# Six modulation vectors of a two-block network made in earlier stages

## The chip, the cores and the metric

The kernel runs on one core of a Trainium2 chip. The metric is the device time of one execution in microseconds (us); lower is better. TensorE is called PE in the views, VectorE DVE, ScalarE ACT, GpSimd POOL and SyncE SP.

## What is computed

512 tokens of 1024 channels, batch 1, go through two blocks of two layers each. Every layer is modulated by vectors that come from one conditioning row: `cond @ w` with a 1024 x 1024 piece of a weight matrix for each vector. They don't depend on the tokens, so each can be made at any time before its use.

```python
def first_block(...):                    # layer 0: even_mixer (MLA and window), layer 1: odd_mixer (diff and forgetting)
    cond = jax.nn.silu(c)
    for layer in range(DEPTH):           # DEPTH = 2
        mod = cond @ w_ada[layer] + b_ada[layer]
        shift, scale, gate = jnp.split(mod, 3, axis=-1)
        h = rmsnorm(x, g_pre[layer]) * (1.0 + scale[:, None, :]) + shift[:, None, :]
        y = even_mixer(h, ...) if layer % 2 == 0 else odd_mixer(h, ...)
        x = x + gate[:, None, :] * rmsnorm(y, g_post[layer])
    return x

def second_block(...):                   # layer 0: conformer_conv, layer 1: hgrn2_mixer
    cond = jax.nn.silu(c)
    for i in range(DEPTH):
        mod = (cond @ ada_w[i] + ada_b[i]).astype(x.dtype)
        sh1, sc1, g1, sh2, sc2, g2 = jnp.split(mod, 6, axis=-1)
        h = modulate(rms_norm(x, norm1_g[i]), sh1, sc1)
        y = conformer_conv(h, ...) if i % 2 == 0 else hgrn2_mixer(h, ...)
        x = x + g1[:, None, :] * y
        h = modulate(rms_norm(x, norm2_g[i]), sh2, sc2)
        a = jax.nn.relu(h @ mlp_w1[i])   # 1024 x 4096
        x = x + g2[:, None, :] * ((a * a) @ mlp_w2[i])
    return rms_norm(x, final_g)
```

## The kernel before

The stages follow one another: even attention, odd attention, convolution, first MLP, recurrent mixer ("hgrn"), second MLP. All activations stay in SBUF, transposed, as a pair of high and low parts (`hTh`, `hTl`); a product in float32 is the sum of three products of such parts (`mm3`, lines 206 to 208). Weights are loaded by SyncE in granules of 512 KB (`wgran`, lines 210 to 226, the load at line 214). They go into one of four `raw` buffers and are split into one of five `hl` buffers: the high part on ScalarE (line 222), the low part on VectorE or GpSimd (line 225). The MLP goes through four quarters of 1024 hidden units. A quarter is w1 and then w2. w1 is done by `gemm_q`, which multiplies in seven block products instead of eight: it sums weight blocks (line 1211), splits them (lines 200 and 201), multiplies (line 1231), and VectorE adds the products (line 1224). w2 is done by plain products, and VectorE multiplies their sums by the gate (line 1145). The first half of quarter 0's w1 is done by plain products, too.

A modulation vector is made by `ada` (line 485) in eight steps, four for each half of its 1024 columns. A step loads 512 KB of the weight matrix (line 495, on SyncE's queue) into one of two buffers `araw`, or in the recurrent stage into one of the four `raw`. One step later VectorE multiplies and adds them into `acc` in two operations of 128 x 512 (line 546, the first of a half line 544). After four steps TensorE sums `acc` over the partitions in a block of eight small products (line 552). VectorE adds the bias (line 554) and, for a scale or a gate with a norm weight, one more operation (line 507), and SyncE writes the half to DRAM in four rows (line 510). In the convolution TensorE does the products itself. Where a vector is used, `spread` (line 588) loads it for all partitions.

`ada` only puts the eight steps on the list `pend`. `group` (line 571) is called for every finished group of outputs, and at every `tick_every`-th call it takes one step from the list; `flush` (line 581) takes all that are left. A scheduler then sets the order of each engine's instructions. It may place a step's instructions earlier than where they were issued, as far as buffers and a marked gate allow. Each engine and each queue does its list in order.

The lines that the change touches are in `first` (the odd attention), `second` (convolution and recurrent stage), `mlp` and the part of `build` ahead of the first MLP. Other names: in the attentions line 637 reads scores into the softmax, line 640 is its reciprocal, line 644 GpSimd's scaling, lines 623 and 625 are rope, line 709 adds a part of the output `o`, line 204 splits a transposed part `b`, and line 654 transposes. In the recurrent stage `X` (lines 1593 and 1596) is a step of the scan.

## Time and profile before

| | |
|---|---|
| runs, median of 3 | 2077.5 us (2074.36 to 2078.72) |
| the profiled execution, its own time | 2076.88 us |
| its span in the profile | 2075.1 us |
| mean granted clock of TensorE | 0.969 of full speed |
| TensorE busy | 1950.8 us, 94% of the span |
| VectorE busy | 1322.0 us, 64% |
| ScalarE, GpSimd busy | 881.2 us (42%), 741.7 us (36%) |
| bytes moved by DMA | 272.13 MB |

The span is the time from the first to the last instruction in the trace; it is 1.8 us shorter than the execution's own time. Stages, from the lines of their instructions: odd attention to about 700 us, with its mixer from 407 to 690; convolution to about 985; first MLP from there to 1336; recurrent stage to about 1700; second MLP from about 1711 to the end. Of a window the columns are its length, then the busy time (and number of instructions) of PE, PEld (weight loads of TensorE), DVE, ACT and POOL, the granted clock of TensorE as a share of its upper level, the busy share of DMA, and GB/s.

### The profile page before, as it was taken

How to read it: one execution, taken by the hardware profiler on the slowest of the kernel's cores; microseconds unless marked ns; L12 is line 12 of the kernel's file. 1: busy time of each engine (PE TensorE's matmuls, PEld its weight loads, DVE VectorE, ACT ScalarE, POOL GpSimd, SP SyncE). 2: the span in 40 equal slices, each digit the busy share in tenths (PEclk: the TensorE clock that was granted, in tenths of full speed). 3: DMA queues.
4: the chain of work that ended last, by engine and by line, in shares of the span. 5: the costliest groups of instructions: out<-in, count | busy, mean ns of one | idle time of the engine just before them, and what ended most of it. 6: DMA issues, size and time to landing. Idle time of an engine off the chain costs nothing.

```text
span 2075.1 us, 33235 instructions
## 1 busy us (share of the span) xinstructions
PE 1950.8 (94%) x13047; PEld 1591.7 (77%) x13047; DVE 1322.0 (64%) x1976; ACT 881.2 (42%) x1497; POOL 741.7 (36%) x671
## 2 busy tenths in 40 slices
PE   7799999699999999879899999999999998999998
PEld 5687767677766787448788989877787678898896
DVE  4356674467553369646988658557677858475673
ACT  3345543135543441142525436244566534353452
POOL 1233344233233233005232422446586543323222
PEclk9899979899999999999999999999999999999999
DMA  8484456377761335832554234452423422242331
GB/s 309 135 211 154 134 163 167 80 176 165 117 148 51 134 116 184 225 88 92 175 169 146 80 113 153 141 158 88 117 75 114 133 82 82 82 133 72 122 103 60
DMA packets 229972, 272.13 MB, mean 131 GB/s; under 512 B 26810, under 2 KB 154009, under 8 KB 229816
## 3 DMA queue, kind: packets, MB, share of 16 engines
q1 hardware_dynamic: 192054, 232.83, 38.9%
q10 hardware_dynamic: 37762, 37.18, 6.1%
q8 instruction: 103, 1.69, 0.3%
q14 instruction: 53, 0.43, 0.1%
HBM read 253.57 MB, written 16.40 MB: 130 GB/s over the span
## 4 chain that ended last, share of the span: by engine, by line
PE 46%; DVE 8%; issue 4%; DMA 3%; ACT 1%; POOL 1%; ACTq 0%; POOLq 0%; SPq 0%; DVEq 0%
PE mm L208 26%; PE mm L1231 5%; PE sc L208 4%; PE sc L1231 4%; PE tp L1231 3%; DVE ol L1351 2%; DMA ud<-u 1%; DVE hl L201 1%; DVE acc L546 1%; PE pv L208 1%; DVE hl L225 1%; DMA u<-ud 1%; PE tp L609 0%; POOL xr L1756 0%; PE sc L1370 0%
## 5 line engine op out<-in xcount | busy, mean ns | idle before, releaser
L208 PE MATMUL mm<-hTh,hl 128*128 128x512 f32 (+2 forms) x1200 | 371.7, 384 | 0.1
L222 ACT CAST hl<-raw 128x1024 fp32r<-128x1024 f32 (+3 forms) x219 | 224.2, 1034 | 238.5 <-PE mm L208 117.8
L208 PE MATMUL mm<-hl,hid 128*128 128x512 f32 x1344 | 317.2, 395 | 3.6 <-DVE hid L201 2.0
L208 PEld LDWEIGHTS mm<-hl,hid 128*128 128x128 f32 x1344 | 251.8, 188 | 63.5 <-DVE hid L201 3.0
L225 DVE TENSOR_TENSOR hl<-raw,hl 128x1024 fp32r<-128x1024 f32 (+2 forms) x187 | 243.1, 1309 | 55.6 <-ACT hl L222 47.7
L208 PEld LDWEIGHTS mm<-hTh,hl 128*128 128x128 f32 (+1 forms) x1200 | 218.0, 188 | 48.7 <-issue 6.5
L208 PE MATMUL mm<-hl,hTh 128*128 128x256 f32 (+3 forms) x848 | 218.5, 339 | 29.2 <-DVE t L625 21.2
L208 PE MATMUL mm<-hTl,hl 128*128 128x512 f32 (+2 forms) x600 | 229.4, 383 | 0.1
L1148 POOL TENSOR_TENSOR xr<-xr,t 128x512 f32<-128x512 f32 x56 | 80.7, 1441 | 306.3 <-DVE t L1145 304.5
L208 PEld LDWEIGHTS mm<-hl,hTh 128*128 128x128 f32 x848 | 152.0, 200 | 46.6 <-issue 15.8
L644 POOL TENSOR_TENSOR s<-s,sm 128x256 f32<-128x256 f32 (+3 forms) x112 | 81.2, 726 | 200.3 <-DVE sm L640 193.0
L546 DVE SCALAR_TENSOR_TENSOR acc<-araw,ccol,acc 128x512 f32<-128x512 f32 x154 | 134.5, 873 | 26.7 <-DMA araw<-in_ada_w_dram 20.7
L200 ACT CAST hl<-raw 128x1024 fp32r<-128x1024 f32 x84 | 86.9, 1048 | 138.3 <-PE mm L208 111.9
L208 PE MATMUL mm<-hl,hTl 128*128 128x256 f32 (+3 forms) x424 | 142.4, 336 | 0.6 <-DVE hTl L458 0.6
L201 DVE TENSOR_TENSOR hl<-raw,hl 128x1024 fp32r<-128x1024 f32 x84 | 131.4, 1579 | 13.7 <-ACT hl L200 13.1
L208 PEld LDWEIGHTS mm<-hTl,hl 128*128 128x128 f32 (+1 forms) x600 | 113.1, 189 | 21.8 <-issue 1.4
L1211 POOL TENSOR_TENSOR raw<-raw,raw 128x1024 f32<-128x1024 f32 x28 | 77.0, 2749 | 142.9 <-DVE rows L1211 89.0
L225 POOL TENSOR_TENSOR hl<-raw,hl 128x1024 fp32r<-128x1024 f32 x32 | 79.4, 2483 | 100.8 <-ACT hl L222 100.8
L639 ACT ACTIVATE s<-s,sm 128x256 f32<-128x256 f32 (+5 forms) x128 | 69.6, 543 | 90.6 <-DVE sm L637 83.5
L1145 DVE TENSOR_TENSOR t<-mm,rows 128x512 f32<-128x512 f32 x56 | 38.5, 688 | 107.4 <-PE mm L208 107.1
L208 PE MATMUL sc<-b,b 64*128 64x256 f32 (+7 forms) x384 | 92.0, 356 | 1.7 <-DVE sm L637 1.2
L1596 POOL TENSOR_TENSOR X<-X,T 128x512 f32<-128x512 f32 x56 | 75.8, 1358 | 44.6 <-ACT op L1556 32.1
(366 smaller groups left out, 4036.0 us busy)
## 6 DMA issues: line engine op xcount, KB each, us to landing
raw<-in_mlp_w_dram SPq DMA_DIRECT2D x128, 512.0 KB
araw<-in_ada_w_dram SPq DMA_DIRECT2D x72, 512.0 KB
raw<-in_hgrn_w_in_dram SPq DMA_DIRECT2D x40, 512.0 KB
araw<-in_w_ada_dram SPq DMA_DIRECT2D x32, 512.0 KB
raw<-in_od_w_in_dram SPq DMA_DIRECT2D x32, 512.0 KB
raw<-in_ada_w_dram SPq DMA_DIRECT2D x24, 512.0 KB
rows<-row SPq DMA_DIRECT2D x16, 512.0 KB
raw<-in_conv_w_in_dram SPq DMA_DIRECT2D x16, 512.0 KB
```

The source lines that it names most:

```text
L200: nc.scalar.copy(out=hi, in_=src)
L201: nc.vector.tensor_tensor(out=lo, in0=src, in1=hi.bitcast(F32), op=ALU.subtract)
L208: self.nc.tensor.matmul(out, lhsT=lt[a], rhs=rt[b], start=start and n == 0, stop=stop and n == 2)
L222: self.nc.scalar.copy(out=hi, in_=raw[:, :n])
L225: eng.tensor_tensor(out=lo, in0=raw[:, :n], in1=hi.bitcast(F32), op=ALU.subtract)
L546: eng.scalar_tensor_tensor(out=acc, in0=raw[:, k], scalar=c, in1=acc, op0=ALU.mult, op1=ALU.add)
L639: nc.scalar.activation(out=s[:, :m], in_=s[:, :m], func=AF.Exp, scale=-1.0, bias=mn, accum_out=sm)
L644: nc.gpsimd.tensor_tensor(out=p, in0=p, in1=r.to_broadcast([P, n]), op=ALU.mult)
L1148: eng.tensor_tensor(out=xs, in0=xs, in1=t, op=ALU.add)
L1211: eng.tensor_tensor(out=out, in0=x, in1=y, op=f)
L1231: nc.tensor.matmul(ps[:, m * 256:m * 256 + 256], lhsT=ws[n][:, a, k, m * P:m * P + P], rhs=parts[n][b][:, k], start=m + k + t == 0, stop=m ...
L1596: nc.gpsimd.tensor_tensor(out=xk, in0=xk, in1=cap(Tt, 1, [(row - 1, 2), (2, nb), (0, hh)]), op=ALU.mult)
```

## The change

The three vectors of the recurrent mixer (scale, shift and gate of `wa2[1]`, 24 steps) were on the list of the first MLP. They are put on that of the odd attention, which then has seven vectors instead of four. There a step is now taken at every finished group instead of every second (`TO`). The three vectors of the second MLP (scale, shift and gate, 24 steps) were on the list of the recurrent stage; they are put on that of the first MLP. There no step is taken during quarter 0, and one at every second group from quarter 1 on. The list isn't flushed at the MLP's end: four steps are left to the recurrent stage.

```diff
@@ -55,7 +55,7 @@
 TE = 2
 NP = 24
 G2 = 2
-TO = 2
+TO = 1
 SQ = 3
 TV = 0
 TVE = 3
@@ -1254,6 +1254,7 @@
         nc = self.nc
         for q in range(4):
             hid = {}
+            self.tick_every = 2 if q else 1000
 
             def pair(n):
                 if n not in hid:
@@ -1679,6 +1680,9 @@
                         rows += [k.ada(cc2, wa2[0], ba2[0], 1024, "scale", h["norm1_g_2"][0]),
                                  k.ada(cc2, wa2[0], ba2[0], 0, "shift")]
                         mods[0] = [k.ada(cc2, wa2[0], ba2[0], 2048, "gate")]
+                        mods["n1"] = [k.ada(cc2, wa2[1], ba2[1], 1024, "scale", h["norm1_g_2"][1]),
+                                      k.ada(cc2, wa2[1], ba2[1], 0, "shift")]
+                        mods[1] = [k.ada(cc2, wa2[1], ba2[1], 2048, "gate")]
                     if G2 == 2 + i:
                         mods["g2"] = k.ada(cc2, wa2[0], ba2[0], 5120, "gate")
                     o = mixer(act)
@@ -1710,12 +1714,10 @@
                 k.ada_tag = "tq"
                 k.ada_raw = ("raw", 4) if i else ("araw", 2)
                 k.tick_every = 1
-                if i == 0 or AH:
+                if i == 0:
                     rest(i)
                 if i == 0 and G2 == 4:
                     mods["g2"] = k.ada(cc2, wa2[0], ba2[0], 5120, "gate")
-                if i and AH > 1:
-                    mods[1] += [k.ada(cc2, wa2[1], ba2[1], 5120, "gate")]
                 k.tick_every = TE if i else 1
                 k.ada_pe, k.ada_ps = i == 0, "tp"
                 o = mixer(act)
@@ -1771,23 +1773,17 @@
                 if MK & 2:
                     k.mark()
                 g2 = mods["g2"] if G2 else k.ada(cc2, wa2[0], ba2[0], 5120, "gate")
-                rows = [k.ada(cc2, wa2[1], ba2[1], 1024, "scale", h["norm1_g_2"][1]),
-                        k.ada(cc2, wa2[1], ba2[1], 0, "shift")]
-                mods[1] = [k.ada(cc2, wa2[1], ba2[1], 2048, "gate")]
-                if AH < 1:
-                    rest(1)
-                if AH < 2:
-                    mods[1] += [k.ada(cc2, wa2[1], ba2[1], 5120, "gate")]
+                rest(1)
+                mods[1] += [k.ada(cc2, wa2[1], ba2[1], 5120, "gate")]
                 st = {}
 
                 def last(tb):
                     if tb == 0:
-                        k.flush()
-                        st["S"], st["B"] = [k.spread(r) for r in rows]
+                        st["S"], st["B"] = [k.spread(r) for r in mods["n1"]]
                     nc.scalar.dma_start(out=(out if upto == 4 else x4)[tb * P:(tb + 1) * P, :], in_=xr[tb])
                     k.prenorm(k.act, tb, xr[tb], st["S"], st["B"])
 
-                k.mlp(act, h["mlp_w1_2"][0], h["mlp_w2_2"][0], xr, lambda: k.tick(len(k.pend) - NP) or k.spread(g2), last)
+                k.mlp(act, h["mlp_w1_2"][0], h["mlp_w2_2"][0], xr, lambda: k.spread(g2), last)
             if upto == 4:
                 return
         with tc.tile_pool(name="xp", bufs=1, reuse_waits="tile") as k.xp:
```

How the order moves, at three places, all on VectorE.

At the start of the odd attention, ahead of its first output part `o` (line 709) and the first split of a transposed part `b` (line 204), before the change:

```order
L554 TENSOR_TENSOR arow_4109<-mm_4111,arow_4109 128x128
L544 TENSOR_SCALAR acc_4104<-araw_4105,ccol_93 128x512
...
L546 SCALAR_TENSOR_TENSOR acc_4104<-araw_4105,ccol_93,acc_4104 128x512
L546 SCALAR_TENSOR_TENSOR acc_4104<-araw_4176,ccol_93,acc_4104 128x512 x2
L546 SCALAR_TENSOR_TENSOR acc_4104<-araw_4321,ccol_93,acc_4104 128x512
...
L546 SCALAR_TENSOR_TENSOR acc_4104<-araw_4321,ccol_93,acc_4104 128x512
L546 SCALAR_TENSOR_TENSOR acc_4104<-araw_4449,ccol_93,acc_4104 128x512 x2
...
L709 SCALAR_TENSOR_TENSOR o_4180<-o_4180,mm_4294 128x512
...
L204 SCALAR_TENSOR_TENSOR b_972_4246<-tq_4241,b_972_4246 128x512
```

And after it, at the same place:

```order
L544 TENSOR_SCALAR acc_4113<-araw_4114,ccol_93 128x512
...
L546 SCALAR_TENSOR_TENSOR acc_4113<-araw_4114,ccol_93,acc_4113 128x512
L546 SCALAR_TENSOR_TENSOR acc_4113<-araw_4159,ccol_93,acc_4113 128x512 x2
...
L546 SCALAR_TENSOR_TENSOR acc_4113<-araw_4189,ccol_93,acc_4113 128x512 x2
L546 SCALAR_TENSOR_TENSOR acc_4113<-araw_4219,ccol_93,acc_4113 128x512 x2
...
L544 TENSOR_SCALAR acc_4281<-araw_4282,ccol_93 128x512
...
L546 SCALAR_TENSOR_TENSOR acc_4281<-araw_4282,ccol_93,acc_4281 128x512
L546 SCALAR_TENSOR_TENSOR acc_4281<-araw_4384,ccol_93,acc_4281 128x512
...
L546 SCALAR_TENSOR_TENSOR acc_4281<-araw_4384,ccol_93,acc_4281 128x512
L709 SCALAR_TENSOR_TENSOR o_4223<-o_4223,mm_4357 128x512
...
L546 SCALAR_TENSOR_TENSOR acc_4281<-araw_4481,ccol_93,acc_4281 128x512
...
L204 SCALAR_TENSOR_TENSOR b_990_4309<-tq_4304,b_990_4309 128x512
```

Four loads (`araw`) are summed ahead of line 709 before, and ten after; the first four of the ten make up a half that stands ahead of the rows shown. Ahead of line 204 it is four before and twelve after, the twelfth with one of its two operations.

In w1 of the first MLP's quarter 1, before, where `hl` are split weights, `hid` split hidden units, `t` the sums of products:

```order
L1224 TENSOR_TENSOR t_2047_9958<-t_2047_9958,tp_10012 128x512
L554 TENSOR_TENSOR arow_10048<-tq_10050,arow_10048 128x128
L544 TENSOR_SCALAR acc_10043<-araw_10044,ccol_93 128x512
L201 TENSOR_TENSOR hl_10200<-raw_10190,hl_10200 128x1024
L546 SCALAR_TENSOR_TENSOR acc_10043<-araw_10044,ccol_93,acc_10043 128x512
L1211 TENSOR_TENSOR rows_10198<-raw_10194,raw_10196 128x1024
L1224 TENSOR_TENSOR t_2048_9959<-t_2048_9959,mm_10060 128x512
L201 TENSOR_TENSOR hid_10040<-t_2047_9958,hid_10040 128x2x256
L546 SCALAR_TENSOR_TENSOR acc_10043<-araw_10117,ccol_93,acc_10043 128x512
L1224 TENSOR_TENSOR t_2047_9958<-t_2048_9959,sc_10086 128x512
L546 SCALAR_TENSOR_TENSOR acc_10043<-araw_10117,ccol_93,acc_10043 128x512
L546 SCALAR_TENSOR_TENSOR acc_10043<-araw_10152,ccol_93,acc_10043 128x512
```

And after:

```order
L201 TENSOR_TENSOR hl_10253<-raw_10243,hl_10253 128x1024
L1211 TENSOR_TENSOR rows_10251<-raw_10247,raw_10249 128x1024
L1224 TENSOR_TENSOR t_2067_10034<-t_2067_10034,mm_10121 128x512
L201 TENSOR_TENSOR hid_10115<-t_2066_10033,hid_10115 128x2x256
L1224 TENSOR_TENSOR t_2066_10033<-t_2067_10034,sc_10147 128x512
L1224 TENSOR_TENSOR t_2067_10034<-t_2067_10034,tp_10178 128x512 x2
L201 TENSOR_TENSOR hid_10175<-t_2066_10033,hid_10175 128x2x256
L201 TENSOR_TENSOR hl_10258<-raw_10243,hl_10258 128x1024
```

The operations of lines 544, 546 and 554 that stood among the splits and sums are gone from this place.

In w1 of quarter 3, after; before, no modulation operation stands there:

```order
L1224 TENSOR_TENSOR t_2250_11617<-t_2250_11617,tp_11671 128x512
L554 TENSOR_TENSOR arow_11707<-tq_11709,arow_11707 128x128
L544 TENSOR_SCALAR acc_11702<-araw_11703,ccol_93 128x512
L201 TENSOR_TENSOR hl_11851<-raw_11841,hl_11851 128x1024
L546 SCALAR_TENSOR_TENSOR acc_11702<-araw_11703,ccol_93,acc_11702 128x512
L1211 TENSOR_TENSOR rows_11849<-raw_11845,raw_11847 128x1024
L1224 TENSOR_TENSOR t_2251_11618<-t_2251_11618,mm_11719 128x512
L201 TENSOR_TENSOR hid_11699<-t_2250_11617,hid_11699 128x2x256
L546 SCALAR_TENSOR_TENSOR acc_11702<-araw_11807,ccol_93,acc_11702 128x512
L1224 TENSOR_TENSOR t_2250_11617<-t_2251_11618,sc_11745 128x512
L546 SCALAR_TENSOR_TENSOR acc_11702<-araw_11807,ccol_93,acc_11702 128x512
L546 SCALAR_TENSOR_TENSOR acc_11702<-araw_11960,ccol_93,acc_11702 128x512
```

A half's sums now stand among the splits and sums of quarter 3: these, and three more of line 546 behind them.

## Rows read from the trace of the kernel before

**Rows 1.** The page, part 1: busy time, share of the span and count of each engine.

```profile
PE 1950.8 (94%) x13047; PEld 1591.7 (77%) x13047; DVE 1322.0 (64%) x1976; ACT 881.2 (42%) x1497; POOL 741.7 (36%) x671
```

**Rows 2.** Windows of both MLPs: busy (count) by engine, then clock, DMA share, GB/s.

```profile
992.20:1021.90 29.70, 24.17 (x178) 22.86 (x176) 29.70 (x31) 16.49 (x20) 5.99 (x3) 0.89 0.51 162
1021.90:1070.50 48.60, 46.54 (x208) 36.27 (x209) 38.53 (x47) 14.29 (x19) 16.11 (x9) 1.00 0.57 184
1070.50:1118.80 48.30, 44.19 (x353) 42.71 (x352) 46.26 (x52) 25.37 (x34) 14.49 (x4) 0.93 0.58 180
1118.80:1164.00 45.20, 45.20 (x201) 36.28 (x200) 22.10 (x26) 12.29 (x15) 15.25 (x10) 1.00 0.26 85
1249.10:1289.50 40.40, 40.40 (x338) 40.36 (x337) 36.39 (x36) 24.18 (x33) 10.72 (x4) 1.00 0.48 158
1740.90:1768.40 27.50, 22.53 (x171) 22.12 (x170) 26.18 (x25) 18.49 (x25) 7.24 (x3) 0.88 0.37 115
1768.40:1813.00 44.60, 44.60 (x195) 36.16 (x193) 17.67 (x21) 12.17 (x15) 15.14 (x10) 1.00 0.23 71
1813.00:1852.90 39.90, 39.90 (x338) 39.90 (x337) 36.12 (x36) 24.73 (x34) 10.63 (x4) 1.00 0.44 133
```

**Rows 3.** Windows of the first MLP, line 546 alone: VectorE busy (count).

```profile
992.20:1021.90 29.70, 6.56 (x6) 0.89 0.51 162
1021.90:1070.50 48.60, 18.62 (x20) 1.00 0.57 184
1070.50:1118.80 48.30, 9.85 (x11) 0.93 0.58 180
```

**Rows 4.** Windows of the odd, the even and the recurrent stage, columns as in 2.

```profile
407.00:690.00 283.00, 273.87 (x1540) 205.91 (x1540) 157.15 (x369) 127.29 (x263) 94.48 (x83) 0.99 0.58 126
150.00:330.00 180.00, 174.62 (x1042) 129.06 (x1039) 125.60 (x328) 90.47 (x245) 58.59 (x104) 0.91 0.55 154
1336.00:1690.00 354.00, 347.61 (x3265) 272.76 (x3264) 245.49 (x317) 183.69 (x275) 199.06 (x158) 1.00 0.39 119
```

**Rows 5.** Waits of PE, recurrent stage: us in total, times, longest.

```profile
PE tp L1577 <- POOL X L1596: 1.5, 2, 0.9
PE tp L1586 <- DVE X L1593: 1.3, 2, 0.8
```

**Rows 6.** PE by line, line 552, recurrent stage and odd attention.

```profile
L552 PE MATMUL tq<-acc,ones 128*32 128x128 f32 x48 | 3.8, 285 | 0.0
...
L552 PE MATMUL mm<-acc,ones 128*32 128x128 f32 x64 | 3.8, 285 | 0.0
```

**Rows 7.** DVE by line, recurrent stage: busy, mean ns, idle before.

```profile
L546 DVE SCALAR_TENSOR_TENSOR acc<-raw,ccol,acc 128x512 f32<-128x512 f32 x42 | 41.8, 996 | 16.1 <-DMA raw<-in_ada_w_dram 15.5
```

**Rows 8.** DVE by line, odd attention, columns as in 7.

```profile
L546 DVE SCALAR_TENSOR_TENSOR acc<-araw,ccol,acc 128x512 f32<-128x512 f32 x49 | 41.4, 844 | 19.3 <-DMA araw<-in_ada_w_dram 15.0 <-DMA araw<-in_w_ada_dram 4.0
...
L544 DVE TENSOR_SCALAR acc<-araw,ccol 128x512 f32<-128x512 f32 x7 | 6.9, 990 | 0.0
```

**Rows 9.** Waits of PE, even attention from 150 to 330.

```profile
PE tq L654 <- DVE sm L640: 1.5, 1, 1.5
```

**Rows 10.** Waits of PE, odd attention.

```profile
PE mm L208 <- DVE o L709: 1.7, 1, 1.7
PE tp L667 <- POOL s L644: 1.5, 1, 1.5
...
PE tq L654 <- DVE b L204: 1.4, 1, 1.4
```

**Rows 11.** Windows at the start of the odd attention, columns as in 2.

```profile
407.00:420.00 13.00, 12.57 (x94) 12.27 (x95) 7.47 (x14) 3.11 (x5) 6.22 (x5) 0.83 0.49 130
420.00:443.00 23.00, 19.18 (x113) 14.11 (x111) 12.24 (x18) 11.09 (x14) 8.96 (x4) 1.00 0.96 222
```

**Rows 12.** Waits of SyncE's queue, odd attention.

```profile
SPq L214 <- POOL hl L225: 62.4, 10, 25.2
...
SPq L495 <- DVE acc L546: 19.3, 10, 4.9
```

## Prediction

> **What bounds the kernel now.** I read the page first: TensorE is busy for 94% of the span, VectorE for 64% [rows 1]. So the end is set by TensorE's own work and by its gaps, and every added or removed TensorE instruction counts. Then I read time by stages, because the change moves work between stages. The two MLPs run the same code on equal sizes; the first has modulation steps beside it and the second has none, so their difference prices the steps [rows 2]. The first `gemm_q` takes 29.7 us against 27.5, w2 of quarter 0 takes 48.6 against 44.6, w1 of quarter 1 takes 48.3 against 39.9, and w2 of quarter 1 takes 45.2 against 44.6. That makes 15.2 us lost in the first MLP. The first three of these stretches hold 6, 20 and 11 of the multiply-adds L546 [rows 3]. They cost most where VectorE has little to spare: w1 without any has VectorE busy 36.12 of 39.90 us, w2 without any 17.67 of 44.60 [rows 2]. The recurrent stage is another case: TensorE is busy 347.61 of 354 us [rows 4], and its two longest waits add up to 2.8 us [rows 5], though 42 L546 run beside it. In the odd attention VectorE is busy 157.15 of 283 us and DMA's share is 0.58; in the even one they are 125.60 of 180 and 0.55 [rows 4].
>
> **The change part by part.** The number of steps stays the same. 24 of them go from the first MLP to the odd attention, and 20 from the recurrent stage to the first MLP; four stay to be done at the start of the recurrent stage.
>
> *First MLP: about -5.5.* By the order, the first eight of its new 24 steps are done where steps were done before (16 VectorE operations, from the first `gemm_q` to early in w2 of quarter 0), and then none comes until quarter 1's w2. So I leave the 2.2 us of the first `gemm_q`, keep half of the 4.0 of w2 (its 20 operations fall to about 9), and drop all 8.4 of w1 in quarter 1. Four steps in w2 of quarter 1 and four in that of quarter 2 lie in stretches with 27 us of idle VectorE; the 0.6 that quarter 1's w2 loses now is a measure, and I take 0.5 each, which is what a half's TensorE instructions take (0.475, below). The last four steps fall into w1 of quarter 3: seven L546, one L544 and one L554. At the rate of quarter 1's w1 the seven are 7 x 9.85/11 = 6.3 us [rows 3], the L544 1.0 [rows 8], and I leave the L554 out. That is 7.3 us in a stretch where VectorE is busy 36.39 of 40.40 [rows 2]. If the idle 4.0 take their share 3.3 are lost, if not 7.3. Eleven L546 in quarter 1's w1 went with 8.4 lost, so seven would go with 5.3. I take 4.5, between 3.3 and 5.3. What is left is 2.2 + 2.0 + 0.5 + 0.5 + 4.5 = 9.7 of 15.2, so -5.5. The bounds are -1 (w2 of quarter 0 keeps its loss and quarter 3's w1 costs 7.3) and -12 (only the first `gemm_q` and the two halves' 1.0 stay).
>
> *Recurrent stage: about -4.5.* Five of six blocks of eight TensorE instructions L552 leave: 5 x 3.8/6 = 3.2 us [rows 6]. At 98% busy nothing hides them, so that is near the lower bound. VectorE also loses most of the 42 L546 and of the 15.5 us that it sits waiting for their loads [rows 7]. TensorE's two waits for X, 2.8 us, are what these can shorten [rows 5]; I take 1.3. The bounds are -3 and -8, the latter if three quarters of the stage's idle 6.4 us come back with the 3.2.
>
> *Odd attention: about +7.5.* 24 steps come in, at one per finished group of outputs. Six more halves issue 6 x 3.8/8 = 2.9 us of L552 [rows 6]; that part is sure. VectorE gets 42 L546 and 6 L544, by their means here 35.4 + 5.9 = 41 us [rows 8], and is then at 198 of 283, or 70%, just as in the even stage (125.60 of 180) [rows 4], where TensorE's longest wait for VectorE is 1.5 us [rows 9]. So the average is no obstacle. The start is. There TensorE waits 1.7 us for `o` L709 and 1.4 for `b` L204 [rows 10], one after the other on VectorE. By the order four steps stand ahead of either before, and after the change ten ahead of the one and twelve ahead of the other. VectorE does its list in order, so each step delays them, and with them the transposes and the first scores, by its sums and by the wait for its load. The sums: eight steps are 16 x 0.85 = 14 us; VectorE is idle 5.5 of 13 us and then 10.8 of 23 [rows 11], so they just fit. The loads: eight of 512 KB are 4.2 MB, at the 222 GB/s that DMA moves there 19 us, while its share is 0.49 from 407 to 420 and 0.96 from 420 to 443. Free are 13 x 0.51 + 23 x 0.04 = 7.6 us [rows 11], so 11.4 are lacking. Weight loads can give way: SyncE waits 62.4 us for GpSimd's splits to free a weight buffer in this stage [rows 12], so weights come early. I take 40% of the 11.4 as lost, 4.6: the term is 2.9 + 4.6 = +7.5. The bounds are +3 (all of it gives way) and +18 (none does, and the sums of the last two steps, 4 x 0.85 = 3.4, come behind it).
>
> What speaks against the place: an L546 takes a mean of 844 ns here and 996 in the recurrent stage [rows 7, 8], where GpSimd is busy 199.06 of 354 us rather than 94.48 of 283 [rows 4], so the two engines seem to get into each other's way. The Trainium skill, "SBUF — State Buffer", section "SBUF: two separate sides", says that a VectorE operation with two SBUF inputs and a GpSimd operation that reads SBUF shut each other out for the whole instruction; the rows agree in their direction. By that rule each moved operation could also hold up GpSimd's softmax scaling L644; if each of the 48 cost L644 the 0.15 us by which the two means lie apart, and all of that reached TensorE, the odd term would be +15 and the sum +5. I keep +7.5, since the 49 of now leave no larger wait on GpSimd in TensorE's list [rows 10].
>
> *The rest: 0.* The steps of the conv stage, the even attention and the second MLP stay as they are.
>
> **Sum:** -5.5 - 4.5 + 7.5 = -2.5. The profiled execution took 2076.88 us, so 2074.4 for its like; it lies 0.6 under the median of the runs, 2077.5. I predict 2075.0 for the median. About 0.2%, 4.2 us, is what a measurement of this kernel can tell from no change.
>
> **The rivals.**
> *A, a full gain.* The four steps in quarter 3 hide after all, since weights can be split ahead during w2 with its 27 us of idle VectorE, and the odd start loses nothing because weight loads give way. Then the MLP gives 15.2 - 2.2 - 2.0 = 11, the recurrent stage 4.5, and odd costs 2.9: -12.6, or 2065. For it: the idle VectorE of w2 [rows 2] and the small waits of the even stage [rows 9]. Against it: quarter 1's w1, 8.4 us longer with eleven L546.
> *B, the odd start waits for its loads.* A step's load goes into one of two buffers and is issued when the step two before it is summed (SyncE waits 19.3 us for that now [rows 12]), and od_w_in loads stand behind it in the same queue. If nothing gives way the stage loses 18 and the sum is +8: 2085.5. It decides from the point where L204 comes 7 us late, since 2.9 + 7 is what the MLP and the recurrent stage give back; at 11 us late the kernel is slower by more than 0.2%. For it: DMA at 0.96 just there [rows 11], and 4.0 us of waiting for one load in w_ada, 15.0 for six others [rows 8]. Against it: only 23 of the 283 us are so full. The Trainium skill, "DMA: Bandwidth & Descriptors", section "Anatomy of one DMA — SWDGE (gpsimd) path", says that the wait of a DMA on a semaphore is made by the issuing sequencer before dispatch, which is how a load behind it would be held; SyncE's waits agree.
> *C, no effect.* The scheduler hoists steps to where it likes and TensorE is full, so the vectors change place without changing what it waits for: the L552 blocks cancel (five leave, six come, one leaves the MLP) and the time stays 2077.5. The order speaks against it: w1 of quarter 1 has no such operation left.
>
> **How the numbers follow.** The forecast gets 0.40, A 0.22, B 0.27, C 0.11. The range reaches to A and to B, 2064 to 2086, and leaves out about a tenth at each end, where two terms reach their bounds at once. Faster by over 0.2% is below 2073.3: A and a third of the forecast, 0.36. Slower is above 2081.7: B and a little of the forecast, 0.29. Within is what is left, 0.35.
>
> **What would show it.** In the changed profile w1 of quarter 1 should take about 40 us, and w1 of quarter 3 about 45 (40 would be A). The recurrent stage should be 4 to 5 us shorter. In the odd stage the first L709 and L204 should come some 5 us later against the stage's start, with VectorE waiting for `araw` ahead of them; at 11 or more B holds. The prediction is wrong if the odd stage grows by over 18 us, or if quarter 1's w1 stays at 48.

## The result and the profile after

| | before | after | ratio, 95% interval |
|---|---|---|---|
| median of 4 runs | 2078.11 us (2074.36 to 2084.47) | 2110.06 us (2105.94 to 2114.73) | 1.0148, 1.0127 to 1.0169 |
| span of the profiled execution | 2075.1 us | 2107.2 us | |

The kernel is 1.5% slower, 31 us. That lies outside the range, and near no case that I priced; rival B had the place and about a quarter of the size (+8).

I put the spans side by side stage by stage, between the same instructions of TensorE. The odd attention (from TensorE's restart after its one long wait at the first rope, at 407.4 before and 405.4 after, to the last softmax reading, line 637) went from 284.3 to 313.7 us, so +29.4. The first MLP from its first `gemm_q` to the start of quarter 3's w2 went from 297.3 to 296.8. The recurrent stage between two equal products of its start and its end went from 339.6 to 338.0. What is left of the 32.1 us lies elsewhere: -2.0 ahead of the odd attention's restart, +4.2 between its last softmax reading and the first `gemm_q`, +2.5 behind the recurrent stage.

The page, part 1, of the kernel after:

```profile
PE 1959.8 (93%) x13047; PEld 1605.0 (76%) x13047; DVE 1321.3 (63%) x1976; ACT 879.2 (42%) x1497; POOL 743.2 (35%) x671
```

VectorE works no more than before (1321.3 us against 1322.0 in [rows 1]), and TensorE 9 us longer with the same instructions.

Windows of the odd attention as a whole, first before, then after (length, then PE, PEld, DVE, ACT, POOL busy, clock, DMA share, GB/s):

```profile
407.40:691.70 284.30, 274.68 (x1548) 206.48 (x1550) 157.64 (x371) 128.56 (x266) 94.94 (x84) 0.99 0.58 127
```

```profile
405.40:719.10 313.70, 287.07 (x1588) 218.46 (x1590) 196.38 (x425) 128.62 (x266) 100.35 (x84) 0.94 0.65 157
```

VectorE is busy 196.38 of 313.70 us, 63%, and DMA 0.65: neither is full on average, as I had said. TensorE is busy 12.4 us longer and idle 17.0 us longer (26.6 against 9.6). Of the 12.4, six more halves' blocks are 2.9 by [rows 6]; the rest, 9.5, is the same products at a lower granted clock, 0.94 of the upper level instead of 0.99.

The stage is not slower all along. Line 637 reads scores 64 times; split at the 25th of these readings, the same one in both, the two parts are, first before, then after:

```profile
407.40:539.41 132.01, 124.83 (x788) 102.05 (x788) 83.95 (x189) 57.61 (x113) 43.11 (x35) 0.97 0.69 153
539.41:691.70 152.29, 149.85 (x762) 104.43 (x763) 73.68 (x182) 70.95 (x154) 51.82 (x49) 1.00 0.49 104
```

```profile
405.40:568.08 162.68, 138.00 (x813) 113.22 (x814) 107.33 (x224) 57.95 (x113) 46.19 (x35) 0.88 0.71 177
568.08:719.10 151.02, 149.08 (x776) 105.24 (x777) 89.04 (x202) 70.66 (x153) 54.16 (x49) 1.00 0.58 136
```

The first part is 30.7 us longer, the second 1.3 shorter. The first holds 32 steps, one in 5.1 us, where it held 16.5 before. The second holds 19.5 steps in the 110 us to their last sum, one in 5.6, where it held 11.5, and they cost nothing: TensorE is idle for 1.9 us there and at its upper clock. Already before the change the parts differed. In the first VectorE was busy 64% of the time and DMA 0.69, in the second 48% and 0.49. After it the first has 66% and 0.71: it took the added work by getting longer. The second has 59% and 0.58.

Windows of the start, first before, then after, show the idle time and the lower clock together:

```profile
420.00:435.00 15.00, 15.00 (x83) 10.58 (x82) 8.05 (x10) 8.21 (x11) 4.81 (x2) 1.00 0.92 189
```

```profile
420.00:435.00 15.00, 9.95 (x59) 5.90 (x58) 9.81 (x12) 7.43 (x10) 5.39 (x2) 0.84 0.74 207
```

Where TensorE was busy for all of 15 us at the upper level, it is now busy for 9.95 at 0.84 of it.

TensorE's waits in this stage after (us in total, times, longest):

```profile
PE mm L208 <- DVE t L625: 11.3, 2, 10.8
PE mm L552 <- DVE acc L546: 7.1, 2, 5.1
PE tq L654 <- DVE b L204: 6.5, 2, 5.5
PE mm L208 <- DVE o L709: 3.1, 1, 3.1
PE mm L208 <- ACT Vd L977: 2.6, 1, 2.6
```

The first is the wait ahead of the stage, which was 12.9 before. The second is new: TensorE has reached a half's block (line 552) in its list and can't go on until VectorE has done the sums. The third and fourth were 1.4 and 1.7 us in [rows 10].

What VectorE does there, from the timeline (start, length, instruction, then the idle time ahead of it and what ended it):

```profile
421.78 0.49 DVE L544 TENSOR_SCALAR acc<-araw,ccol 128x512 f32<-128x512 f32 x1 [2.85 <-DMA araw<-in_ada_w_dram]
...
430.61 3.50 DVE L546 SCALAR_TENSOR_TENSOR acc<-araw,ccol,acc 128x512 f32<-128x512 f32 x2 [1.29 <-DMA araw<-in_ada_w_dram]
...
442.37 0.49 DVE L544 TENSOR_SCALAR acc<-araw,ccol 128x512 f32<-128x512 f32 x1 [5.71 <-DMA araw<-in_ada_w_dram]
...
447.46 0.68 DVE L709 SCALAR_TENSOR_TENSOR o<-o,mm 128x512 f32<-128x512 f32 x1
...
453.58 0.69 DVE L204 SCALAR_TENSOR_TENSOR b<-tq,b 128x512 fp32r<-128x512 f32 x1
```

The first output part (line 709) comes 42.1 us after the restart; it was 29.0 before (436.4 less 407.4). The three rows of sums shown wait 2.85, 1.29 and 5.71 us for their loads. The first split of a transposed part (line 204) comes 48.2 us after the restart; it was 35.4. Over the whole stage VectorE's waits for the steps' loads are these:

```profile
DVE acc L546 <- DMA araw<-in_ada_w_dram: 28.9, 18, 5.1
...
DVE acc L544 <- DMA araw<-in_ada_w_dram: 17.1, 5, 6.1
```

That is 46.0 us against 19.0 before (15.0 and 4.0 in [rows 8]).

The first MLP after, windows of the first `gemm_q`, w2 of quarter 0, w1 and w2 of quarter 1, w1 of quarter 3, and under it what TensorE waits for in the first of them:

```profile
1023.84:1057.93 34.09, 25.52 (x179) 24.36 (x177) 33.05 (x33) 16.40 (x21) 8.69 (x3) 0.85 0.52 164
1057.93:1105.14 47.21, 45.75 (x200) 36.02 (x199) 23.70 (x30) 14.49 (x18) 14.77 (x10) 1.00 0.33 105
1105.14:1145.02 39.88, 39.88 (x338) 39.87 (x337) 35.87 (x36) 24.46 (x34) 10.63 (x4) 1.00 0.40 132
1145.02:1190.78 45.76, 45.76 (x203) 36.24 (x201) 25.80 (x32) 12.44 (x15) 15.65 (x10) 1.00 0.38 117
1276.42:1320.62 44.20, 41.76 (x347) 40.47 (x346) 41.84 (x45) 24.89 (x34) 13.49 (x4) 1.00 0.49 161
```

```profile
PE sc L1231 <- DVE hl L201: 4.6, 1, 4.6
PE tp L1231 <- DVE hl L201: 4.0, 1, 4.0
```

Against [rows 2], w1 of quarter 1 fell from 48.3 to 39.9, and w2 of quarter 0 from 48.6 to 47.2. But the first `gemm_q` rose from 29.7 to 34.1 with two waits for split weights, w1 of quarter 3 from 40.4 to 44.2, and w2 of quarters 1 and 2 by half a microsecond each.

The recurrent stage, between the same two products, before and after:

```profile
1346.20:1685.80 339.60, 333.21 (x3201) 261.01 (x3199) 233.30 (x302) 180.08 (x269) 193.52 (x152) 1.00 0.38 116
```

```profile
1377.40:1715.40 338.00, 328.80 (x3161) 260.19 (x3160) 198.65 (x252) 179.48 (x269) 191.02 (x152) 1.00 0.27 83
```

TensorE's work fell by 4.4 us, the stage only by 1.6; TensorE's idle time grew from 6.4 to 9.2 us, though VectorE had 35 us less to do.

### The profile page after: what moved, and what is told of

Same layout as the page of the kernel before. It is cut to its first block, busy times and chain, and to the rows that moved or that the text cites. A ratio compares the mean times of both kernels' runs of the same rounds, so it can differ in the third digit from the quotient of the medians.

```text
span 2107.2 us, 33252 instructions
## 1 busy us (share of the span) xinstructions
PE 1959.8 (93%) x13047; PEld 1605.0 (76%) x13047; DVE 1321.3 (63%) x1976; ACT 879.2 (42%) x1497; POOL 743.2 (35%) x671
## 4 chain that ended last, share of the span: by engine, by line
PE 44%; DVE 7%; issue 4%; DMA 3%; ACT 2%; POOL 2%; ACTq 0%; POOLq 0%; SPq 0%; DVEq 0%
PE mm L208 26%; PE mm L1231 4%; PE sc L208 4%; PE sc L1231 3%; PE tp L1231 3%; DVE ol L1352 2%; DMA ud<-u 1%; PE pv L208 1%; DVE hl L201 1%; POOL xr L1758 1%; DVE hl L225 1%; DMA raw<-in_mlp_w_dram 0%; DMA u<-ud 0%; DVE acc L546 0%; PE tp L609 0%
## 5 line engine op out<-in xcount | busy, mean ns | idle before, releaser
L208 PE MATMUL mm<-hl,hTh 128*128 128x256 f32 (+3 forms) x848 | 224.6, 347 | 31.7 <-DVE t L625 20.2
L546 DVE SCALAR_TENSOR_TENSOR acc<-araw,ccol,acc 128x512 f32<-128x512 f32 x189 | 172.1, 911 | 36.6 <-DMA araw<-in_ada_w_dram 33.0
L208 PEld LDWEIGHTS mm<-hl,hTh 128*128 128x128 f32 x848 | 156.8, 206 | 48.9 <-DVE t L625 11.7
L208 PEld LDWEIGHTS mm<-hl,hTl 128*128 128x128 f32 x424 | 87.6, 207 | 8.2 <-DVE hTl L458 1.5
```

What stands on the lines that cost most here:

```text
L208: self.nc.tensor.matmul(out, lhsT=lt[a], rhs=rt[b], start=start and n == 0, stop=stop and n == 2)
L546: eng.scalar_tensor_tensor(out=acc, in0=raw[:, k], scalar=c, in1=acc, op0=ALU.mult, op1=ALU.add)
```

## The experiments

A table first, of all runs. The start is the time from TensorE's restart to the first output part (line 709), the stage that to the last softmax reading; both are positions in the one profiled execution. Kernels with the odd attention as before gave 284.3, 285.7 and 291.4 us for the stage, and those with it as in the change 313.7, 312.6 and 317.8, so differences below some 7 us there say little. The ratio is to the runs of before on the same chip.

| run | start | stage | ratio, 95% interval |
|---|---|---|---|
| before | 29.0 | 284.3 | 1 |
| the change | 42.1 | 313.7 | 1.0148, 1.0127 to 1.0169 |
| odd move alone | 41.7 | 312.6 | 1.0083, 1.0064 to 1.0103 |
| MLP move alone | 29.9 | 285.7 | 0.9964, 0.9952 to 0.9975 |
| doubled pace alone | 42.2 | 300.2 | 1.0085, 1.0058 to 1.0113 |
| start held back | 29.3 | 316.1 | 1.0217, 1.0199 to 1.0234 |
| slow pace, seven vectors | 29.1 | 286.3 | 1.0272, 1.0242 to 1.0303 |
| pace doubled later | 29.1 | 321.7 | 1.0147, 1.0107 to 1.0187 |
| half the bytes | 39.6 | 305.8 | 1.0077, 1.0049 to 1.0104 |
| half the sums | 41.8 | 306.1 | 1.0064, 1.0042 to 1.0086 |
| half of both | 39.5 | 292.5 | 0.9989, 0.9966 to 1.0013 |
| three buffers | 37.1 | 313.0 | 1.0101, 1.0072 to 1.0129 |
| four buffers | 34.8 | 303.4 | 1.0083, 1.0047 to 1.0119 |
| block one step later | 41.2 | 317.5 | 1.0118, 1.0074 to 1.0163 |
| MLP steps in w2, before | 29.9 | 291.4 | 0.9942, 0.9921 to 0.9963 |
| MLP steps in w2, the change | 44.7 | 317.8 | 1.0099, 1.0070 to 1.0128 |

### Which move makes the loss

The odd attention's part alone, with the second MLP's vectors left in the recurrent stage:

```diff
-                if i == 0:
+                if i == 0 or AH:
                     rest(i)
...
+                if i and AH > 1:
+                    mods[1] += [k.ada(cc2, wa2[1], ba2[1], 5120, "gate")]
...
-                rest(1)
-                mods[1] += [k.ada(cc2, wa2[1], ba2[1], 5120, "gate")]
```

> The three recurrent vectors move to the odd attention at the doubled pace, as in the change; the second MLP's three stay in the recurrent stage, and the first MLP has no steps. Theory S (the loss of the change is made at the start of the odd attention, by steps that stand ahead of results there): the odd stage is some 29 us longer as with the change, the first MLP some 13 us shorter, close to the second MLP's times, the recurrent stage as before: about 2094 us. Rival M (the loss is made by what is moved into the first MLP): about 2070.

Measured: 2097.8 us, 16 above before's 2081.89. The odd stage takes 312.6 us, and the first MLP, now without steps, gives back some 12: products of TensorE run 25.7 us late where the odd attention ends and 13.2 late in quarter 1's w2. So the loss comes with the odd move, and M falls. Whether it is made at the start, as S says, this run doesn't tell.

The MLP's part alone, the odd attention as before:

```diff
-TO = 1
+TO = 2
...
-                        mods["n1"] = [k.ada(cc2, wa2[1], ba2[1], 1024, "scale", h["norm1_g_2"][1]),
-                                      k.ada(cc2, wa2[1], ba2[1], 0, "shift")]
-                        mods[1] = [k.ada(cc2, wa2[1], ba2[1], 2048, "gate")]
+                        mods["n1"], mods[1] = rows[1:3], mods[0][:1]
```

> The odd attention as before; the second MLP's vectors made in the first MLP as in the change. The recurrent block's three vectors are left out (the convolution's are used in their place), so 24 steps are missing. Theory S: the first MLP gives nothing back (first gemm_q +4, quarter 1's w1 -8, quarter 3's w1 +4), the recurrent stage 1 to 3: about 2076. My forecast's own terms (-5.5 and -4.5) would give 2068.

Measured: 2074.73 us, 7 below 2081.89. That is between the two figures expected, 2076 and 2068, which are 2 and 10 us below a before of 2078: products run 3.8 us earlier over the first MLP and 2.7 over the recurrent stage. So this part of the change is no loss, and with the 24 steps left out a small gain.

### Pace or volume in the odd attention

The doubled pace alone, with the four vectors of before:

```diff
-TO = 2
+TO = 1
```

> Only TO goes from 2 to 1: the odd attention has its four vectors, taken at the doubled pace, so that the same twelve steps stand ahead of the first softmax as with the change, and none is added. Theory S: the start loses the same as with the change, some 13 us and the lower clock behind it: 2090 to 2098. Rival V (the volume of 24 more steps costs, wherever they stand): 2078 within 3 us.

Measured: 2097.6 us, 16 above 2081.89, and the start takes 42.2 us as in the change. No step was added; the twelve steps only stand ahead of the first softmax instead of four. V falls as the whole explanation: of the stage's 29 us some 16 come with the pace and some 13 more with the added vectors. That is read from one execution each, and the one profiled here, 2088.66 us, is the lowest of six that go up to 2107.18. In it all 28 steps of the stage fall within 131 us of the restart, one in 4.7. To the 25th reading it takes 151.6 us, 19.6 more than before; behind it, where no step is left, 148.6, 3.7 less.

The change with the steps held back until behind the forget-gate product:

```diff
+        te, self.tick_every = self.tick_every, 1000
         self.run(dqkv(0))
...
         self.gemm_w(act, w, 3072, 8, KC, ev_ff)
+        self.tick_every = te
+        self.mark()
```

> The change, but in the odd attention no step is taken before the forget-gate product, so that the sums stand behind the first output part. Theory S: the start's waits go, and the odd stage is 5 to 12 us longer than before rather than 29: 2085 to 2093. Rival V: the same steps are pressed into less time, so 2110 or more.

Measured: 2126.32 us, 44 above 2081.89. The start is mended (29.3 us), but the stage still takes 316.1 us, and six steps that are left run behind the last softmax and make it later still. Rival V had 2110 or more. So the start is one place of the loss, not its cause: pressed into what remains, the steps cost more. S, which bound the loss to the start, falls here.

The change at the old pace, so that the rest of the list is flushed at the mixer's end:

```diff
-TO = 1
+TO = 2
```

> The change with TO back at 2: seven vectors in the odd attention, the start's order as before the change, and what isn't taken by the end of the mixer flushed there (23 sums behind the last softmax). Theory R: the first output part comes 29 us after the stage's start as before; the end loses by the flush, 10 to 25 us: 2085 to 2100 where before is 2080. If the loss at the start were not from the pace: 42 us and 2105 or more.

Measured: 2140.21 us, 59 above 2081.61, much over the 10 to 25 us of loss by the flush that I gave. The mixer is as before the change (start 29.1, stage 286.3). All of the loss lies behind it; TensorE's waits from the last softmax to 815 us:

```profile
PE mm L552 <- DVE acc L546: 42.2, 5, 10.5
PE mm L208 <- DVE t L756: 4.0, 3, 2.8
```

At the old pace steps are hidden; those that don't fit cost 42 us in five blocks, with nothing beside them.

The change with the old pace to the forget-gate product and the doubled one from there:

```diff
+        te, self.tick_every = self.tick_every, 2
         self.run(dqkv(0))
...
         self.gemm_w(act, w, 3072, 8, KC, ev_ff)
+        self.tick_every = te
```

> The change with the odd attention's pace at every second group until the forget-gate product and at every group from there on; 3 sums stand behind the last softmax. Theory R: the start as before (29 us to the first output part), then the added steps cost what 24 more steps cost in the middle: TensorE's blocks 3 us, waits and clock 5 to 10: 2086 to 2093 where before is 2080. Rival V (the volume makes the loss): 2103 or more.

Measured: 2110.43 us, 29 above 2081.61, as much as the change. The start is mended again, and the waits come later, on softmax results and on transfers for the transposes:

```profile
PE tp L667 <- DVE s L1045: 14.8, 2, 10.2
...
PE tq L654 <- DMA t<-dqk: 10.7, 2, 9.6
```

The longest of them, 10.2 us, is held by a step. VectorE waits 14.07 us for the step's load, and the softmax result stands behind the sum in its list:

```profile
608.06 0.75 DVE L546 SCALAR_TENSOR_TENSOR acc<-araw,ccol,acc 128x512 f32<-128x512 f32 x1 [14.07 <-DMA araw<-in_ada_w_dram]
...
609.77 0.75 DVE L1045 SCALAR_TENSOR_TENSOR s<-s,sm,s 128x512 f32<-128x512 f32 x1
```

I expected 6 to 13 us of loss; the time is rival V's, 2103 or more. So a mended start doesn't make the pace free, and this wait even lies behind the 25th reading. That the pace is dear everywhere doesn't follow: in the change itself the steps behind that reading cost nothing. The added steps put into that part alone were not tried.

### What a step costs there

Half the bytes of each step in the odd attention's seven vectors:

```diff
+            if cut == 1:
+                nc.sync.dma_start(out=raw[:, 0], in_=w[gk * 256:gk * 256 + P, o0:o0 + 512])
+                return raw
...
-                    eng.scalar_tensor_tensor(out=acc, in0=raw[:, k], scalar=c, in1=acc, op0=ALU.mult, op1=ALU.add)
+                    eng.scalar_tensor_tensor(out=acc, in0=raw[:, k * (cut != 1)], scalar=c, in1=acc, op0=ALU.mult, op1=ALU.add)
```

> The change, but a step of the odd attention's seven vectors loads 256 KB and uses them twice (half of their weights is left out, the sums are as many). Theory B (bytes: DMA is full at the start): the first output part comes at about 438 to 440 against a start at 405, the odd stage is 10 us or more shorter than with the change: 2090 to 2098 where before is 2079. Rival (the sums and the order hold it): 2104 or more.

Measured: 2098.66 us. The first output part comes 39.6 us after the restart, 2.5 sooner than in the change, and the stage takes 305.8. Theory B had 33 to 35 us there and a stage at least 10 us shorter, so it falls for the start; its time came, 2090 to 2098 for a before 2 us lower. Bytes are a part; at the start they are not what holds it.

Half the sums, the loads whole:

```diff
-            for k in range(2):
+            for k in range(1 if cut == 2 else 2):
```

> The change, but a step of the odd attention's seven vectors sums only one of its two 128-row pieces (half of the products are left out, the loads are whole). Theory B (bytes): the first output part stays near 445, 2104 or more where before is 2079. Rival (the sums): 2090 to 2098.

Measured: 2094.21 us, start 41.8, stage 306.1. The time is the rival's. The same again: a part, and nothing at the start. Twelve steps stood ahead of the first softmax in all of these orders.

Both halves:

```diff
-            for k in range(2):
+            for k in range(1 if cut == 1 else 2):
```

> The change, with half the bytes and half the sums of the odd attention's seven vectors (half of their weights is left out); the count of steps, their blocks on TensorE and their chain over two buffers stay. Theory W (the loss is the steps' work, bytes and sums together): the odd stage falls from 314 us to 292 or less, 2086 or less where before is 2080. Rival R (it is the chain of round trips, load after sum after load): 300 us or more, 2094 or more, as with either half alone.

Measured: 2078.78 us, no difference from before's 2079.85, and a stage of 292.5 us. So W holds for the stage: with half of the work in 24 added steps and the 32 old ones, the loss is gone. These 56 half steps load and sum less than the 32 whole ones of before, so the run ties the loss to the work, and doesn't tell what the number of steps costs by itself. By the stage either half alone gave 8 us and both gave 21, by the ratios 15 and 17 of the change's 31, and both 33. The ratios add up and the stages don't, and the difference is within the spread of the stages. Whether one resource holds the step where the other is relieved is not shown. At the start the rival is right: it still takes 39.5 us, and TensorE waits 8.6 us for the first output part:

```profile
PE mm L208 <- DVE o L713: 8.6, 1, 8.6
```

Three buffers for the loads instead of two:

```diff
-        self.ada_tag, self.ada_raw = "mm", ("araw", 2)
+        self.ada_tag, self.ada_raw = "mm", ("araw", 3)
```

> The change with three buffers for the steps' loads instead of two (nothing else). Theory R (round trips: a load is issued when the step two before it is summed and takes 6 to 11 us to land, so the steps ahead of the first output part go in a chain, whatever their bytes or sums): with three in flight the first output part comes 36 to 39 us after the stage's start rather than 42, and the odd stage is 5 to 10 us shorter: 2098 to 2105 where before is 2080. Rival (the order alone): 42 us again and 2108 or more.

Measured: 2104.44 us; start 37.1, as theory R has it, but stage 313.0, where R had 5 to 10 us less than the change. Undecided, so four buffers (the same edit with a 4; in both runs the other uses of these buffers got the same number):

> The change with four buffers for the steps' loads instead of two. Theory R (round trips): more loads in flight than with three, the first output part 33 to 37 us after the start and VectorE's waits for loads at half of the change's 46 us; the odd stage 300 us or less, 2096 or less where before is 2080. Rival W (the work): within 4 us of the run with three buffers, 2104.

Measured: 2096.58 us, start 34.8, stage 303.4. The start and the waits for loads are R's, time and stage just miss its 2096 and 300; W's time, within 4 us of 2104, is missed by more. VectorE's waits for loads are 1.5 us instead of 46.0, and yet the stage is 19 us longer than before. What took their place, VectorE's and then TensorE's waits of this run:

```profile
DVE acc L546 <- DMA araw<-in_ada_w_dram: 1.5, 1, 1.5
```

```profile
PE tq L654 <- DMA t<-dqk: 8.5, 1, 8.5
PE mm L552 <- DVE acc L546: 3.6, 1, 3.6
PE tq L654 <- ACT hn L1109: 3.2, 1, 3.2
```

```profile
408.80:712.20 303.40, 281.96 (x1588) 214.51 (x1590) 199.89 (x425) 128.54 (x266) 97.00 (x84) 0.94 0.68 163
```

With more loads in flight TensorE waits 8.5 us for a transfer of the attention's own (`t` from `dqk`), where DMA's share is 0.68 rather than 0.65, and its clock stays at 0.94. The chain over two buffers is some 10 us of the 29 (13 of 31 by the ratios). The rest stays with the loads landed in time, so it isn't the chain; the run with half of both ties it to the steps' work.

TensorE's block of a half issued one step later, with two accumulators:

```diff
+            self.ada_late.append(lambda: total(half, acc))
+
+        def total(half, acc):
             arow = bias(half)
```

> The change, with TensorE's block of eight products of a half issued one step later, so that TensorE doesn't reach it before its sums are done (a second accumulator buffer). Theory T (TensorE, in order, is held by the block that waits for sums that wait for loads): the 7 us of waiting at line 552 at the start of the odd attention go, and with the clock 7 to 15 us: 2097 to 2105 where before is 2079. Rival L (VectorE's own list is late): the waits move to the output part and the transposed part, 2108 or more.

Measured: 2107.81 us, start 41.2, stage 317.5. The waits at the block are gone from TensorE's list in this stage (7.1 us in the change), and nothing is gained that is clear of the noise: the ratio's interval overlaps the change's, and the stage is no shorter. The time lies between T's and L's. L holds in that the waits move, though to other places than it named:

```profile
PE tq L657 <- DMA t<-dqk: 6.1, 1, 6.1
PE sc L208 <- DVE sm L640: 5.8, 2, 3.5
```

The second accumulator also let the scheduler take one more half ahead of this stage (96 sums in it instead of 104), so the order differs by more than the block. The block is where TensorE meets the late sums, not why they are late.

### Where steps are cheap in the MLP

The kernel before, with the first MLP's steps taken in w2 of quarters 0 to 2 alone:

```diff
             hid = {}
+            self.tick_every = 1000
...
+            self.tick_every = 1
+            self.mark()
             if q == 0:
                 mk = self.acc_x(xr, G())
```

> The kernel before, with the first MLP's 24 steps taken in w2 of quarters 0 to 2 alone, one per finished group, and not to be scheduled ahead of it. Theory P (a step costs by the place where its sums stand): first gemm_q 27.5, every w1 40, each of three w2 about 1 us over the second MLP's 44.6, so 12 to 13 us off the first MLP: 2066 to 2069 where before is 2079. Rival (the 24 steps cost by their number): within 4 us of before.

Measured: 2070.55 us, 10.6 below 2081.13. This version beats both kernels. Its windows of the first `gemm_q`, w2 of quarter 0, w1 and w2 of quarter 1, w1 of quarter 3:

```profile
1002.20:1029.60 27.40, 22.37 (x170) 22.17 (x169) 27.02 (x25) 19.08 (x26) 6.16 (x3) 0.88 0.41 123
1029.60:1075.30 45.70, 45.70 (x203) 36.30 (x201) 33.32 (x35) 11.80 (x15) 14.92 (x9) 1.00 0.48 148
1075.30:1115.62 40.32, 40.32 (x338) 40.32 (x337) 36.62 (x38) 25.73 (x35) 11.68 (x4) 1.00 0.43 133
1115.62:1161.35 45.73, 45.73 (x211) 36.32 (x210) 33.00 (x39) 11.33 (x14) 16.86 (x10) 1.00 0.53 164
1246.94:1286.81 39.87, 39.87 (x337) 39.87 (x336) 35.60 (x35) 24.21 (x33) 10.63 (x4) 1.00 0.48 156
```

All stand within half a microsecond of the second MLP's times [rows 2] but for 1.1 us in each w2, of which 0.95 is what two blocks take. The first MLP takes 284.6 us instead of 297.3, so theory P holds. The same 24 steps lost 15.2 us where they stood before, 10.6 of it in the first `gemm_q` and quarter 1's w1.

The same edit in the changed kernel:

> The change with the first MLP's steps taken in w2 of quarters 0 to 2 alone, as in the run that did so with the kernel before; the odd attention as in the change. Theory P: the first gemm_q falls from 34 to 28 us, quarter 3's w1 from 44 to 40, w2 of the quarters 0 to 2 stay at 46 to 47, so 9 to 11 us come off the first MLP: 2099 to 2102 where before is 2080. Rival (the first gemm_q is late from the convolution's end, whatever stands in it): 2105 or more.

Measured: 2102.56 us, some 10 below the change by the two ratios (1.0099 against 1.0148). The first `gemm_q` takes 29.0 us, quarter 3's w1 40.3, and the MLP 286.7 instead of 296.8. So the steps that the scheduler hoisted into the first `gemm_q` made most of what its 34.1 lies over the second MLP's 27.5. In the run with the MLP move alone five L546 stand in it instead of seven, and it takes 28.8.

## Why the prediction was wrong

**The odd attention, +7.5: the step that failed.** I took the average for safe ("So the average is no obstacle") by likeness to the even stage, looked for the loss at the start alone, and so put all steps behind the start at nothing. The average hid two unlike parts. The first, to the 25th softmax reading, had VectorE at 64% and DMA at 0.69 without the added steps; it got 15.5 of them and 30.7 us longer. The second, at 48% and 0.49, took the other eight for nothing. The start did lose, 13 us rather than 4.6, inside the bound of 18, but only as the head of that first part: the runs with the start mended kept the loss, and the one with half of both kinds of work lost it. VectorE and DMA can be near 70% and still be late for what is asked of them in order, and TensorE then waits for that. The even stage takes 32 steps in 180 us, one in 5.6, and TensorE's longest wait for VectorE there is 1.5 us [rows 9]; what it would take without steps, and why it bears that pace, was not tried.

**"That part is sure": the six blocks, 2.9 us.** Their own time was sure, their place in TensorE's list was not costed: TensorE waited 7.1 us there for sums. With the block moved the waits stood at other lines.

**The clock was missing.** 9.5 us of TensorE's longer work is the granted clock of 0.94, and no term of mine held it, though [rows 11] show 0.83 in the stretch after the stage's wait. How much of it the added waits cause is open. The kernel with the MLP's steps in w2 has the odd attention of before, and nearly its idle time, 10.2 us, but a clock of 0.96, and TensorE is busy there 6.5 us longer than before:

```profile
408.70:700.10 291.40, 281.18 (x1548) 210.78 (x1550) 158.09 (x370) 129.02 (x266) 94.97 (x84) 0.96 0.57 124
```

The three kernels with the change's odd attention all have 0.94, those with the old one 0.96 to 0.99.

**The first MLP, -5.5.** The part on quarter 1's w1 came out (39.9 us), and so did quarter 3's w1 (44.2 against my 45). The step that failed is "I leave the 2.2 us of the first `gemm_q`": 4.4 us were added there. The order shows about as many operations as before; their seven L546 took 8.92 us where six had taken 6.56 [rows 3], and the splits behind them came late twice. Of w2 in quarter 0, 2.6 us were left rather than 2.0. The sum is -0.5.

**The recurrent stage, -4.5.** TensorE's 4.4 us of work left, near my 3.2, and idle time came back for it, 2.8 us. "At 98% busy nothing hides them" was wrong: here, of 4.4 us of work that left a busy engine, 1.6 were gained. What takes the 2.8 us is not shown by a run.

**The rivals.** B named the mechanism, and priced it at 18 by looking at 36 us of the stage; it has the start right and nothing of the rest. By the signs that I gave, line 204 came 12.8 us later, over the 11 at which B holds, and the stage grew by more than 18. (My sum for 11 us late is +3.9, just short of the 4.2 that I called slower.) A's condition, weight loads that give way, didn't decide anything: no wait for weights stands among TensorE's larger ones. Of the port rule that I weighed, the mean of L546 in the changed odd stage is 908 ns against 844, in its direction. GpSimd's busy time in the stage grew by 5.4 us for the same 84 instructions (94.94 to 100.35), near the 48 x 0.15 = 7.2 priced, but TensorE's list of waits in the changed stage has none on GpSimd (1.5 us before [rows 10]), so it didn't reach TensorE by that way. What the longer sums cost on VectorE, no run sets apart.

## What to carry to other kernels

Work put under a busy engine is priced stretch by stretch, by the pace at which each can take it, not by the average share of the engines over a stage. First look where along the stage the same instructions fall behind, and change the pace alone, with nothing added, to see what that costs. Place the work where the helper engine has idle time within the stretch itself, and hold it there against the scheduler: 24 steps cost 15 us spread over w1 and w2, and 3 in w2 alone. Cost an instruction that a change puts into an in-order list by what it may wait for, and compare TensorE's clock as well as its waits.

## What was not expected of the hardware

The clock: the same odd attention was granted 0.99 of the upper level in one kernel and 0.96 in another with nearly the same idle time, 6.5 us of TensorE's time apart. And a load's landing: with half the bytes, a load of 256 KB was issued at 433.0 and summed at 444.0, with VectorE idle for the last 6.3 us of that, while DMA's share was 0.62:

```profile
433.03 1.98 SPq L497 DMA_DIRECT2D araw<-in_ada_w_dram  x2
```

```profile
444.03 0.49 DVE L548 TENSOR_SCALAR acc<-araw,ccol 128x512 f32<-128x512 f32 x1 [6.30 <-DMA araw<-in_ada_w_dram]
```

```profile
435.00:450.00 15.00, 8.64 (x51) 7.38 (x48) 8.46 (x12) 4.80 (x7) 2.04 (x1) 0.89 0.62 138
```

Two weight granules of 512 KB had been issued just ahead of it on the same queue; whether they held it was not tried.
